# Dense stages: the weight split placed behind a step's transpositions, and the second pair scaled in two steps

## Chip, cores and metric

The kernel runs on one core of one Trainium2 chip. The metric is the device time of one execution in microseconds (us); the time before is the median of three runs. One further execution was recorded by the hardware profiler; all durations below come from it. Five engines work side by side, each through its own list of instructions in order: TensorE (PE: matrix products and transpositions, results in PSUM), VectorE (DVE), ScalarE (ACT), GpSimd (POOL) and SyncE (SP, which issues most transfers). They wait for one another by semaphores.

## The reference

An encoder of two layers over 1024 tokens of width 1024, in fp32: layer 0 mixes tokens by a 2-D neighbourhood attention, layer 1 by a grouped-query attention. The change lies where the output projection of a mixer ends and the gate product begins:

```python
        x = x + y
        g = jax.nn.sigmoid(rms_norm(x, ple_norm_g[i]) @ ple_w_gate[i])
        x = x + g * (p[i] @ ple_w_proj[i])
    return rms_norm(x, final_norm_g)
```

`rms_norm(x, g)` is x times the reciprocal root of the mean of its squares, times a gain. y is the mixer's output; its last step is the output projection, `(o * jax.nn.silu(gate)) @ w_out`.

## The kernel before

**Numbers in two parts.** Every matrix product is made of three: each operand is split into a high part (a rounded copy, made on ACT) and a low part (operand less high part, made on DVE), and `split3` (its matmuls stand at L352) adds high x high, high x low and low x high. HTh and HTl are the two parts of the transposed activations, tile t of 128 tokens in eight chunks of 128 columns; wh and wl are those of one unit of weights (128 x 1024), whose raw form lies in a staging tile (wstage, two of them).

**The dense stage** (`dense_phase`, once behind each mixer, so twice in the program) does the output product, the residual, a norm, and the gate product. The output product is a Strassen form of seven products instead of eight (`strassen_out`). Its last part is a loop of eight steps, numbered n = 0 to 7 here, which `dense_phase` drives at L1831. In a step PE does one block of twelve 128x512 matmuls; then DVE adds the block's PSUM tile to half of a tile X of the residual (`fold`, L1691), ACT squares that half and sums it (`square`, L1777), and these follow in the order written:

- `WQ.pump()`: DVE makes the low part wl of the weight unit begun one pump earlier (`settle`, L246), SP issues the load of a further unit, and ACT makes the high part wh of the next unit (L241). Here the units are the four of the gate product's first half.
- `norms[n]`: pieces of the norm. `prep` (L1807, n = 1), `powers` (L1787 and a power on POOL, n = 2, 4, 7), `roots` (L385 to L387, n = 3, 5, 8), `scale_pair` (L1802, n = 3, 5, 9, 11), which writes the normed tiles xn of two token tiles m and 4 + m. Pair 0 (tiles 0 and 4) is scaled in step 3 as four pieces of 512 columns, pair 1 (tiles 1 and 5) in step 5 as two whole tiles of 1024.
- `pend_ht(True)`: up to two entries of a list are taken. Each one (`to_ht`, L530) is four PE transpositions of 128 columns from xn into one of four PSUM tiles t (L534), a copy to HTh on ACT (L535) and the subtraction into HTl on DVE (L536). An entry is due three steps behind its scaling for the first half of the columns, four for the second. So PE has a group of eight transpositions, four of each tile of a pair, behind the blocks of steps 5 and 6 (pair 0), 7 and 8 (pair 1), then 11 and on.

Steps from n = 8 on belong to the gate product (L1930 and on); blocks 8 and 9 use weight units 0 and 1 with the first halves of token tiles 0 and 4, blocks 10 and 11 units 2 and 3 with their second halves. That loop is not touched.

**What sets the order.** The program is scheduled by hand: each engine gets its instructions in the order in which the Python code issues them, and takes them strictly in that order.

Of the kernel before, what the change touches and what calls it, by code (L numbers as in the profile page):

```python
# [16 lines left out]
ALU = mybir.AluOpType  # L17
# [148 lines left out]
def trunk(ctx, tc, x, wts, rpb, gains, hgains, mask, sides, rope, gain0, out):  # L166
    nc = tc.nc
    sync, act, dve, pool, pe = nc.sync, nc.scalar, nc.vector, nc.gpsimd, nc.tensor
# [125 lines left out]
    WQ = Weights()  # L294
# [213 lines left out]
    def load_gain(pl, i, bufs):  # L508
        gt = pl.tile([128, D], F32, name="gain", bufs=bufs)
        sync.dma_start(gt, bcast(gains, i * D, D))  # L510
        return gt
# [18 lines left out]
    def to_ht(pt, t, xn, cs=(0, 1)):  # L530
        for c in cs:
            ps = pt.tile([128, 4, 128], F32, name="t")
            for k in range(4):
                pe.transpose(ps[:, k], xn[:, (4 * c + k) * 128:(4 * c + k + 1) * 128], ident)  # L534
            act.activation(HTh[:, t, 4 * c:4 * c + 4], ps, AF.Copy)  # L535
            dve.tensor_tensor(HTl[:, t, 4 * c:4 * c + 4], ps, HTh[:, t, 4 * c:4 * c + 4], ALU.subtract)  # L536
# [1205 lines left out]
    def dense_phase(l):  # L1742
        with ExitStack() as es:
# [4 lines left out]
            X = [one.tile([128, D], F32, name=f"X{t}") for t in range(NT)]  # L1748
# [10 lines left out]
            def xalloc():  # L1759
                return sb.tile([128, D], F32, name="xn", bufs=4)  # L1760

            def salloc():
                return stg.tile([128, D], F32, name="wstage")

            def pend_ht(pairs=False):
                clock[0] += 1
                for _ in range(2 if pairs else 1):
                    if pend and pend[0][0] <= clock[0]:
                        to_ht(ps_t, *pend.pop(0)[1:])
# [4 lines left out]
            def square(t, c):  # L1774
                i = 2 * (t % 4) + t // 4
                cs = slice(512 * c, 512 * c + 512)
                act.activation(junk[:, cs], X[t][:, cs], AF.Square, accum_out=sa[:, c, i:i + 1])  # L1777

            rn = {}
# [11 lines left out]
            def roots(m, k):  # L1791
                r = sb.tile([128, 4], F32, name="rn", bufs=4)[:, :2 * k]
                root_step(r, *half_roots.pop(m))
                for i in range(k):
                    rn[m + i] = r[:, 2 * i:2 * i + 2]

            def scale_pair(m, age=3):
                xs = [(t, xalloc()) for t in (m, 4 + m)]
                n = 512 if m == 0 else 1024
                for c in range(0, 1024, n):  # L1800
                    for i, (t, xn) in enumerate(xs):
                        dve.scalar_tensor_tensor(xn[:, c:c + n], X[t][:, c:c + n], rn[m][:, i:i + 1], g1[:, c:c + n],  # L1802
                                                 op0=ALU.mult, op1=ALU.mult)
                pend.extend([(clock[0] + age + c, t, xn, (c,)) for c in range(2) for t, xn in xs])

            def prep():
# [3 lines left out]
                1: [prep],  # L1810
                2: [lambda: powers(0, 1)],
                3: [lambda: roots(0, 1), lambda: scale_pair(0)],
                4: [lambda: powers(1, 1)],
                5: [lambda: roots(1, 1), lambda: scale_pair(1)],
                7: [lambda: powers(2, 2)],
                8: [lambda: roots(2, 2)],
                9: [lambda: scale_pair(2)],
                11: [lambda: scale_pair(3)],
            }
# [11 lines left out]
            for n, (step, m) in enumerate(strassen_out(l, X, ps_d, ps_t, early)):  # L1831
                if n == 0:
                    sb = es.enter_context(tc.tile_pool(name="dsb", bufs=2))
                    wp4 = es.enter_context(tc.tile_pool(name=f"wp4{l}", bufs=2))
                    WQ.alloc[4] = lambda: [wp4.tile([128, 1024], F32R, name=f"w{c}4") for c in "hl"]
                    WQ.cap[4] = 2
                    g1 = load_gain(sb, 2 * l + 1, 2)
                    g2 = load_gain(sb, 2 * l + 2, 2)
                    WQ.age, WQ.lag, age, lag = 1, 0, WQ.age, WQ.lag
                square(m + 4 if step == 5 else m, 1)  # L1840
                WQ.pump()
                for f in norms.get(n, ()):
                    f()
                pend_ht(True)
            WQ.age, WQ.lag = 2, 2

            for kind in ("ple",):
# [3 lines left out]
                for hf in range(2):  # L1851
# [77 lines left out]
                    for t, i in order:  # L1929
# [31 lines left out]
                        xn = salloc() if l == 0 and t >= 6 else xalloc()  # L1961
# [40 lines left out]
    ropeD = dram.tile([2, NT, 128, 2, 64], F32, name="ropeD")  # L2002
    mixer_a()
    pend = dense_phase(0)
    mixer_b(pend)
    dense_phase(1)


# [16 lines left out]
```

## Time and profile before

| | us |
|---|---|
| Median of 3 runs (lowest to highest) | 1480.99 (1480.89 to 1481.51) |
| The profiled execution's time | 1481.56 |
| Its span, first to last instruction | 1479.8 |
| ACT busy in the span | 914.3 (62%) |
| POOL busy in the span | 430.7 (29%) |

The first dense stage's eight steps lie at about 571 to 594 us of the span, the second's at about 1360 to 1383. In a row of the timeline the first number is the start in us from the span's start, the second how long the row lasts; then engine, line, operation, tile written <- tiles read, shape, and how many instructions the row holds; in brackets is the idle time ahead of it on its engine, and who ended it. A PE instruction's recorded time runs into the next one's, so PE's pace is read from start to start.

### The profile page before, as it was taken

The numbers are of one execution on the slowest core, as the hardware profiler recorded it, in microseconds if no ns is written. First come the engines' busy times: TensorE is split into PE (matmuls) and PEld (weight loads), VectorE is DVE, ScalarE is ACT, GpSimd is POOL, SyncE is SP. The second block draws the span as 40 slices with busy tenths as digits, with TensorE's granted clock in tenths as the row PEclk, the third lists the DMA queues.
The fourth block names the chain that finished last, engine by engine and source line by source line (L and its number), as shares of the span: only waits on it lengthen the run. The fifth ranks groups of instructions, "written<-read, shape, count | busy, mean of one in ns | idle before, by whom it ended". The sixth has DMA issues, their size and how long they took to land.

```text
span 1479.8 us, 23443 instructions
## 1 busy us (share of the span) xinstructions
PE 1467.4 (99%) x8305; PEld 1272.1 (86%) x8305; DVE 1071.4 (72%) x1943; ACT 914.3 (62%) x1836; POOL 430.7 (29%) x623
## 2 busy tenths in 40 slices
PE   9999999999999999999999999999999999999997
PEld 7888888988988887888888888999999988888886
DVE  5468776487487598656767787877878787789845
ACT  5477776477477635443456777777767777744522
POOL 3245764275244200020154342424141400000010
PEclk9999999999999999999999999999999999999999
DMA  7324564373122863262120111101101122763223
GB/s 248 116 89 160 108 161 139 72 167 98 36 90 86 327 256 100 86 197 102 61 86 12 40 51 46 42 17 55 46 28 60 42 65 65 256 242 108 78 93 129
DMA packets 91605, 157.62 MB, mean 107 GB/s; under 512 B 18272, under 2 KB 54368, under 8 KB 90976
## 3 DMA queue, kind: packets, MB, share of 16 engines
q1 hardware_dynamic: 87776, 144.71, 29.2%
q0 software_dynamic: 2560, 8.39, 3.7%
q10 hardware_dynamic: 1152, 3.02, 0.7%
q8 instruction: 66, 1.08, 0.3%
q14 instruction: 51, 0.42, 0.1%
HBM read 125.56 MB, written 50.83 MB: 119 GB/s over the span
## 4 chain that ended last, share of the span: by engine, by line
PE 58%; DVE 2%; ACT 1%; issue 0%; POOL 0%; ACTq 0%; POOLq 0%; DVEq 0%
PE d L352 29%; PE s L352 11%; PE o L352 9%; PE t L1446 7%; PE t L534 1%; PE t L352 1%; PE t L1398 0%; DVE xn L1802 0%; DVE X L1691 0%; DVE wl L1589 0%; DVE PTl L1449 0%; DVE mn L1428 0%; DVE HTl L1637 0%; ACT junk L1777 0%; DVE X L1644 0%
## 5 line engine op out<-in xcount | busy, mean ns | idle before, releaser
L352 PE MATMUL d<-wh,HTh 128*128 128x512 f32 (+1 forms) x800 | 285.5, 358 | 0.3 <-ACT G L688 0.2
L352 PE MATMUL d<-wh,HTl 128*128 128x512 f32 (+1 forms) x800 | 282.7, 355 | 0.2 <-DVE HTl L536 0.2
L352 PE MATMUL d<-wl,HTh 128*128 128x512 f32 (+1 forms) x800 | 281.6, 354 | 0.2 <-DVE stat L942 0.2
L1449 DVE TENSOR_TENSOR PTl<-t,PTh 128x512 fp32r<-128x512 f32 x256 | 164.6, 685 | 105.1 <-ACT PTh L1448 104.5
L352 PE MATMUL d<-HTh,wh 128*128 128x512 f32 x480 | 193.8, 404 | 0.0
L352 PE MATMUL d<-HTh,wl 128*128 128x512 f32 x480 | 188.7, 393 | 0.0
L352 PE MATMUL d<-HTl,wh 128*128 128x512 f32 x480 | 188.1, 392 | 0.0
L352 PEld LDWEIGHTS d<-wh,HTh 128*128 128x128 f32 x800 | 150.5, 189 | 22.7 <-ACT G L688 0.5
L352 PEld LDWEIGHTS d<-wh,HTl 128*128 128x128 f32 x800 | 150.8, 189 | 22.3 <-DVE HTl L536 0.5
L352 PEld LDWEIGHTS d<-wl,HTh 128*128 128x128 f32 x800 | 150.8, 189 | 22.3 <-POOL wl L261 0.5
L1434 ACT ACTIVATE P<-s,mn 128x1024 f32<-128x1024 f32 x128 | 143.0, 1117 | 37.8 <-DVE mn L1428 36.7
L1448 ACT ACTIVATE PTh<-t 128x512 fp32r<-128x512 f32 x256 | 138.6, 594 | 43.4 <-PE t L1446 42.1
L1428 DVE TENSOR_REDUCE mn<-s 128x1 f32<-128x1024 f32 x128 | 154.8, 1209 | 5.7 <-PE s L352 5.3
L886 POOL TENSOR_TENSOR PTh<-PTh,SIDE 128x256 fp32r<-128x256 f32 x96 | 80.8, 842 | 201.9 <-ACT PTh L881 201.9
L352 PE MATMUL s<-KA,QS 128*128 128x512 f32 (+2 forms) x384 | 134.8, 405 | 0.0
L1446 PE MATMUL t<-ident,P 128*128 128x128 f32 x1024 | 133.3, 273 | 0.4 <-DVE PTl L1449 0.4
L1446 PEld LDWEIGHTS t<-ident,P 128*128 128x128 f32 x1024 | 116.7, 141 | 9.6 <-DVE PTl L1449 2.1
L352 PE MATMUL s<-KB,QS 128*128 128x512 f32 (+2 forms) x384 | 121.4, 370 | 0.0
L352 PE MATMUL o<-PTl,V 128*128 128x256 f32 (+2 forms) x672 | 119.9, 290 | 0.0
L352 PE MATMUL o<-PTh,V 128*128 128x256 f32 (+2 forms) x672 | 118.1, 287 | 0.7 <-DVE Y L557 0.3
L246 DVE TENSOR_TENSOR wl<-wstage,wh 128x1024 fp32r<-128x1024 f32 x75 | 92.4, 1235 | 27.4 <-ACT wh L241 27.2
L352 PEld LDWEIGHTS d<-HTh,wl 128*128 128x128 f32 x480 | 90.1, 188 | 20.3
(296 smaller groups left out, 2911.4 us busy)
## 6 DMA issues: line engine op xcount, KB each, us to landing
wstage<-in_wts SPq DMA_DIRECT2D x87, 512.0 KB
pp<-ppD SPq DMA_DIRECT2D x32, 256.0 KB
X<-in_x SPq DMA_DIRECT2D x15, 512.0 KB
rb<-rD SPq DMA_DIRECT2D x58, 128.0 KB
tD0t<-in_wts SPq DMA_DIRECT2D x16, 256.0 KB
tD1t<-in_wts SPq DMA_DIRECT2D x16, 256.0 KB
ppD<-th SPq DMA_DIRECT2D x16, 256.0 KB
xD<-X SPq DMA_DIRECT2D x8, 512.0 KB
```

Source lines behind the costliest of these rows:

```text
L246: eng.tensor_tensor(lo[:, c:c + n], s[:, c:c + n], hi[:, c:c + n], ALU.subtract)
L352: pe.matmul(ps, a, b, start=first, stop=last, skip_group_check=True)
L534: pe.transpose(ps[:, k], xn[:, (4 * c + k) * 128:(4 * c + k + 1) * 128], ident)
L886: pool.tensor_tensor(pt[:, 3 * j - 1:3 * j + 4:4], pt[:, f1:f1 + 1].to_broadcast([128, 2, 128]), SIDE[:, :2], ALU.mult)
L1428: dve.tensor_reduce(mn, ps, axis=AX.X, op=ALU.min)
L1434: act.activation(p, ps, AF.Exp, bias=mn, scale=-1.0, accum_out=RS[h, hf][:, t:t + 1])
L1446: pe.transpose(ps[:, i], p[:, k * 128:(k + 1) * 128], ident)
L1448: act.activation(PTh[:, ks, c], ps, AF.Copy)
L1449: dve.tensor_tensor(PTl[:, ks, c], ps, PTh[:, ks, c], ALU.subtract)
```

## The change

In each of the eight steps the pump comes last, behind the step's norm pieces and its transpositions. And of pair 1 only tile 1 is scaled in step 5; the scaling of tile 5 is put off to step 6, behind that step's transpositions and ahead of its pump. No instruction is added or taken away, and the entries for the transpositions keep their steps.

```diff
--- before.py
+++ after.py
@@ -1794,13 +1794,22 @@
                 for i in range(k):
                     rn[m + i] = r[:, 2 * i:2 * i + 2]
 
+            rest = []
+
             def scale_pair(m, age=3):
                 xs = [(t, xalloc()) for t in (m, 4 + m)]
                 n = 512 if m == 0 else 1024
+
+                def scaled(i, c):
+                    t, xn = xs[i]
+                    dve.scalar_tensor_tensor(xn[:, c:c + n], X[t][:, c:c + n], rn[m][:, i:i + 1], g1[:, c:c + n],
+                                             op0=ALU.mult, op1=ALU.mult)
                 for c in range(0, 1024, n):
-                    for i, (t, xn) in enumerate(xs):
-                        dve.scalar_tensor_tensor(xn[:, c:c + n], X[t][:, c:c + n], rn[m][:, i:i + 1], g1[:, c:c + n],
-                                                 op0=ALU.mult, op1=ALU.mult)
+                    for i in range(2):
+                        if m == 1 and i == 1:
+                            rest.append(lambda: scaled(1, 0))
+                        else:
+                            scaled(i, c)
                 pend.extend([(clock[0] + age + c, t, xn, (c,)) for c in range(2) for t, xn in xs])
 
             def prep():
@@ -1838,10 +1847,14 @@
                     g2 = load_gain(sb, 2 * l + 2, 2)
                     WQ.age, WQ.lag, age, lag = 1, 0, WQ.age, WQ.lag
                 square(m + 4 if step == 5 else m, 1)
-                WQ.pump()
+                more = rest[:]
+                del rest[:]
                 for f in norms.get(n, ()):
                     f()
                 pend_ht(True)
+                for f in more:
+                    f()
+                WQ.pump()
             WQ.age, WQ.lag = 2, 2
 
             for kind in ("ple",):
```

PE's list and SP's list hold the same instructions in the same order as before, and so does POOL's. The order changes on DVE and ACT alone, in the same way in both dense stages; shown is the first (X_5832 to X_5839 are the residual's tiles 0 to 7; the numbers on wh and wl are those of tile allocations, rising in the order of the weight units).

On DVE in steps 1 to 3 (the rows of L1691 are the folds of steps 2 and 3):

```order
+L1816 TENSOR_SCALAR sa<-sa 128x8
 L246 TENSOR_TENSOR wl_6307<-wstage,wh_6306 128x1024
-L1807 TENSOR_SCALAR sa<-sa 128x8
 L1691 TENSOR_TENSOR X_5832<-d,X_5832 128x512
-L246 TENSOR_TENSOR wl_6328<-wstage,wh_6327 128x1024
 L1787 SCALAR_TENSOR_TENSOR sa<-sa 128x2
+L246 TENSOR_TENSOR wl_6329<-wstage,wh_6328 128x1024
 L1691 TENSOR_TENSOR X_5838<-d,X_5838 128x512
```

`prep` moved ahead of the first unit's wl, and the sum of `powers` in step 2 ahead of the second unit's wl, which now stands right ahead of the fold of step 3.

On DVE from the roots of step 5 to the fold of step 7 (the first two rows are `roots` of step 5, L1691 with X_5834 is the fold of step 6; the pairs of L536 are the HTl of steps 5 and 6):

```order
 L386 SCALAR_TENSOR_TENSOR wkn<-wkn,sa 128x2
 L387 SCALAR_TENSOR_TENSOR rn<-wkn 128x2
-L1802 SCALAR_TENSOR_TENSOR xn<-X_5833,rn,gain 128x1024
-L1802 SCALAR_TENSOR_TENSOR xn<-X_5837,rn,gain 128x1024
+L1805 SCALAR_TENSOR_TENSOR xn<-X_5833,rn,gain 128x1024
 L536 TENSOR_TENSOR HTl<-t,HTh 128x512 x2
 L1691 TENSOR_TENSOR X_5834<-d,X_5834 128x512
-L246 TENSOR_TENSOR wl_6409<-wstage,wh_6408 128x1024
 L536 TENSOR_TENSOR HTl<-t,HTh 128x512 x2
+L1805 SCALAR_TENSOR_TENSOR xn<-X_5837,rn,gain 128x1024
+L246 TENSOR_TENSOR wl_6430<-wstage,wh_6429 128x1024
 L1691 TENSOR_TENSOR X_5835<-d,X_5835 128x512
```

The scaling of tile 5 (X_5837) moved from behind that of tile 1 to behind four HTl and a fold; the third unit's wl moved behind it.

On ACT from the square of step 5 to that of step 7 (the rows of L1777):

```order
 L1777 ACTIVATE junk,sa<-X_5839 128x512
-L241 ACTIVATE wh_6408<-wstage 128x1024
-L535 ACTIVATE HTh<-t 128x512 x2
+L535 ACTIVATE HTh<-t 128x512 x2
+L241 ACTIVATE wh_6429<-wstage 128x1024
 L1777 ACTIVATE junk,sa<-X_5834 128x512
-L241 ACTIVATE wh_6448<-wstage 128x1024
-L535 ACTIVATE HTh<-t 128x512 x2
+L535 ACTIVATE HTh<-t 128x512 x2
+L241 ACTIVATE wh_6462<-wstage 128x1024
 L1777 ACTIVATE junk,sa<-X_5835 128x512
```

In steps 5 and 6 the high part of a weight unit, wh, moved from ahead of the two HTh copies to behind them.

## The prediction

> **What bounds the kernel now.** First the page's span and its busy line, then the list of who waited for whom, cut to PE and to the first dense stage's steps.
>
> ```profile
> span 1479.8 us, 23443 instructions
> PE 1467.4 (99%) x8305; PEld 1272.1 (86%) x8305; DVE 1071.4 (72%) x1943; ACT 914.3 (62%) x1836; POOL 430.7 (29%) x623
> PE t L534 <- DVE HTl L536: 0.6, 2, 0.4
> ```
>
> PE is busy 99% of the span, so any time that PE stands still in the change's stages is added to the end, and any wait taken away comes off it. The third row is all that the trace names as PE waiting in the first stage: 0.6 us, for HTl to free a PSUM tile. In the second stage the same list is empty. So there is little to win; the question is what PE waits for afterwards. The chain of waits shows how that 0.6 us arises in the first stage:
>
> ```profile
> 592.16 0.95 ACT wh L241
> 593.11 0.49 ACT HTh L535
> 593.60 0.02 issue
> 593.62 0.70 DVE HTl L536
> 594.33 0.04 issue
> 594.37 1.25 PE t L534 x8
> ```
>
> The split of a weight unit (wh) stands on ACT ahead of the HTh copy, DVE's HTl follows, and PE's group of step 8 waits for the PSUM tile. From the end of a DVE instruction (594.32) to PE it takes 0.05 us. PE's timeline, first stage, then second:
>
> ```profile
> 590.20 1.25 PE L534 MATMUL t<-ident,xn 128*128 128x128 f32 x8 [0.36 <-DVE HTl L536]
> 591.21 0.48 PE L352 MATMUL d<-wh,HTh 128*128 128x512 f32 x1
> 595.38 0.47 PE L352 MATMUL d<-wh,HTh 128*128 128x512 f32 x1
> ...
> 1378.80 1.04 PE L534 MATMUL t<-ident,xn 128*128 128x128 f32 x8
> 1379.59 0.48 PE L352 MATMUL d<-wh,HTh 128*128 128x512 f32 x1
> 1383.24 0.48 PE L352 MATMUL d<-wh,HTh 128*128 128x512 f32 x1
> ```
>
> In the second stage the group of step 7 takes 0.79 us (1378.80 to 1379.59), and block 8 with its group 3.65 (1379.59 to 1383.24): this is the pace without waits. In the first stage the same two take 1.01 and 4.17, and 0.36 is lost ahead of them. So the first stage loses 0.36 + 0.22 + 0.52 = 1.1 us here, the second nothing.
>
> **The change part by part.** Nothing is added or removed; everything is a matter of when DVE and ACT reach an instruction. DVE's timeline in the second stage, and ACT's:
>
> ```profile
> 1364.51 1.23 DVE L246 TENSOR_TENSOR wl<-wstage,wh 128x1024 fp32r<-128x1024 f32 x1 [2.27 <-ACT wh L241]
> 1366.33 1.22 DVE L246 TENSOR_TENSOR wl<-wstage,wh 128x1024 fp32r<-128x1024 f32 x1
> 1367.46 0.15 DVE L1787 SCALAR_TENSOR_TENSOR sa<-sa 128x2 f32<-128x2 f32 x1
> 1368.48 0.16 DVE L385 TENSOR_TENSOR wkn<-wkn 128x2 f32<-128x2 f32 x1 [0.26 <-POOL wkn L376]
> 1369.07 2.74 DVE L1802 SCALAR_TENSOR_TENSOR xn<-X,rn,gain 128x512 f32<-128x512 f32 x4
> 1371.72 0.69 DVE L1691 TENSOR_TENSOR X<-d,X 128x512 f32<-128x512 f32 x1
> 1373.26 0.16 DVE L1787 SCALAR_TENSOR_TENSOR sa<-sa 128x2 f32<-128x2 f32 x1 [0.85 <-ACT junk L1777]
> 1373.33 0.69 DVE L1691 TENSOR_TENSOR X<-d,X 128x512 f32<-128x512 f32 x1
> 1374.82 2.48 DVE L1802 SCALAR_TENSOR_TENSOR xn<-X,rn,gain 128x1024 f32<-128x1024 f32 x2
> 1377.21 1.28 DVE L536 TENSOR_TENSOR HTl<-t,HTh 128x512 fp32r<-128x512 f32 x2
> 1378.41 0.68 DVE L1691 TENSOR_TENSOR X<-d,X 128x512 f32<-128x512 f32 x1
> 1379.01 1.22 DVE L246 TENSOR_TENSOR wl<-wstage,wh 128x1024 fp32r<-128x1024 f32 x1
> 1381.38 1.29 DVE L536 TENSOR_TENSOR HTl<-t,HTh 128x512 fp32r<-128x512 f32 x2 [1.15 <-ACT HTh L535]
> ```
>
> ```profile
> 1372.50 0.63 ACT L1777 ACTIVATE junk<-X 128x512 bf16<-128x512 f32 x1 [3.47 <-DVE X L1691]
> 1379.19 0.63 ACT L1777 ACTIVATE junk<-X 128x512 bf16<-128x512 f32 x1 [2.43 <-DVE X L1691]
> 1379.82 1.05 ACT L241 ACTIVATE wh<-wstage 128x1024 fp32r<-128x1024 f32 x1
> 1380.77 1.06 ACT L535 ACTIVATE HTh<-t 128x512 fp32r<-128x512 f32 x2
> ```
>
> The spacings, start to start: wl to the next DVE instruction 1.13 (1366.33 to 1367.46); fold to ACT's square 0.78 (1371.72 to 1372.50); square to `powers` 0.76 (1372.50 to 1373.26); `powers` to the next 0.07; fold to the next 0.60 (1378.41 to 1379.01); `roots` to scaling 0.59 (1368.48 to 1369.07); two whole scalings 2.39 (1374.82 to 1377.21), so one 1.20, and it ends 1.28 after its start; two HTl 1.20 (1377.21 to 1378.41); square to the next on ACT 0.63 (1379.19 to 1379.82); HTh to HTl 0.61 (1380.77 to 1381.38).
>
> *Part 1, the pump behind the norm pieces (steps 1 to 3).* It looks free and is not. Before, DVE made the second unit's wl while ACT squared; now `powers` stands ahead of it, so DVE waits for ACT first and makes wl afterwards. First wl 1364.51; fold of step 2 at 1365.64; square 1366.42; `powers` 1367.18; second wl 1367.25; fold of step 3 at 1368.38; `roots` 1368.98 (POOL's power, at most 1.02 behind `powers`, is there by 1368.20); scaling of pair 0 at 1369.57 instead of 1369.07. So the norm runs 0.50 us later, not earlier. In the second stage PE is past caring: its group of step 5 starts well behind the scaling. If POOL's power should be slower beside a running wl, it has 0.78 us in hand.
>
> *Part 2, tile 5 put off.* From pair 0's scaling to tile 1's the list is unchanged, 5.75 us (1369.07 to 1374.82): tile 1 is scaled at 1375.32. Then HTl of step 5 at 1376.52 (its HTh is early: fold 1373.83, square 1374.61, HTh 1375.24, and HTl could run at 1375.85), fold of step 6 at 1377.72. Here DVE sends ACT to work and needs it back: square 1378.50, HTh of step 6 at 1379.13, HTl 1379.74 and one more, **scaling of tile 5 at 1380.94**, ended 1382.22. Before, it had ended at 1377.30 (1374.82 and 2.48). PE takes tile 5's transpositions in the group of step 7, as before: the group starts at 1378.80, its first four (tile 1) are through at 1379.20, and the second four wait until 1382.27. **The wait is 3.1 us.** Behind it in PE's list stand block 8 and everything after; PE reaches block 8 at 1382.7 instead of 1379.59.
>
> In the first stage DVE begins this list at
>
> ```profile
> 576.65 1.23 DVE L246 TENSOR_TENSOR wl<-wstage,wh 128x1024 fp32r<-128x1024 f32 x1 [2.27 <-ACT wh L241]
> ```
>
> that is 787.86 us ahead of the second stage's 1364.51. The same steps end tile 5's scaling at 594.36; PE goes on at 594.41, the last four transpositions take 0.40, block 8 and its group 3.65: block 9 starts at 598.5 instead of 595.38, **3.1 us later**. PE itself stands still for some 3.8 us there: the group starts at about 590.2 as before, its first four are through at 590.6, and the next comes at 594.41. The 1.1 us lost before lie inside, so they are not lost again.
>
> *Part 3, wh behind HTh on ACT.* This does what the chain above suggests: HTh comes 0.95 us sooner after its square, and PSUM tiles come free sooner (HTl of step 6 at 1379.74 instead of 1381.38). It takes away the first stage's 1.1 us, which is already counted, since the 3.1 compares block 9 with block 9. What is late next is the weights: units 2 and 3 are read by block 10. The third wl follows tile 5 at 1382.14, then the fold of step 7 (1383.27), square (1384.05), `powers` (1384.81), HTl (1385.3 and 1385.9), last wl 1386.5 to 1387.7. Block 10 starts at about 1389.1 now that PE waits: 1.4 us in hand, so I cost it at nothing. Without that cover it is up to the same 1.4 us again. SP's loads keep their order; the buffer for the fourth unit comes free 0.9 us later (wl at 1367.25 instead of 1366.33), its wh runs at 1380, over ten us later.
>
> Sum of the waits: 3.1 + 3.1 = **6.2 us**.
>
> *Part 4, PE's clock in a wait.* No wait of this length lies inside the trace before, so its price is bounded. The end of the run shows PE after its last matmul, and the stretches of the span show the granted clock (the column ahead of the last two):
>
> ```profile
> 1.35 1.97 PE L968 MATMUL gain<-ident 128*128 128x128 f32 x8 [1.35 <-POOL ident masks.py:199]
> 7.15 0.66 PE L534 MATMUL t<-ident,X 128*128 128x128 f32 x4 [0.17 <-DVE X L960]
> 1471.97 0.28 PE L352 MATMUL d<-wh,HTl 128*128 128x256 f32 x1
> 1472.00:1474.00 2.00, 0.24 (x3) 0.05 (x1) 1.39 (x5) 1.90 (x5) 0.00 (x0) 1.00 0.57 231
> 1474.20:1474.40 0.20, 0.00 (x0) 0.00 (x0) 0.05 (x1) 0.12 (x1) 0.00 (x0) 0.50 0.03 0
> ```
>
> The last matmul ends at 1472.25, and from 1474.2 the clock is half: **two us of standing still were enough** once. And it does not come back at once: at the start eight transpositions took 1.97 us, against 1.04 at 1378.80, and the pace was full only by 7.15, 5.8 us after the first one. So after a wait of 3 us or more the work may run at half pace for between 0 and 5.8 us, which loses 0 to 2.9 us in a stage. I take the middle, 1.45 a stage, **2.9 in all**: the end of the run is the nearest row and speaks for a loss, and how long it lasts is open. Below nothing it cannot be.
>
> [...]
>
> Together 6.2 + 2.9 = 9.1 us. Against the profiled execution's own 1481.56 that is 1490.7; that execution lies 0.57 above the median of the three runs, and on the median it is 1480.99 + 9.1 = **1490.1 us**.
>
> **The rivals.**
> 1. *The clock stays up.* The waits come as computed, PE resumes at full pace: 1480.99 + 6.2 = 1487.2. For it: the waits are only 3.1 and 3.8 us. Against: the clock at the end of the run.
> 2. *Tile 5 in time, so not slower.* PE waits for nothing, and the first stage's 1.1 us go: 1480.99 - 1.1 = 1479.9, which is within 0.2% (3.0 us, about what a measurement here can tell from no change). It decides at 1379.20: tile 5's scaling would have to end by then instead of 1382.22, 3.0 us sooner. For it: HTh of step 6 could follow PE's group of step 6 closely, as PSUM is ready early. Against: the list above is bound to DVE and ACT handing X and its square to each other, not to PE, and DVE has only 1.4 us of waiting in it behind tile 1.
> 3. *Only one stage waits,* or each half as long, because a handover is quicker where the list has changed: 1480.99 + 3.1 = 1484.1. For it speaks only that my spacings come from other neighbours.
>
> **How the numbers follow.** Waits in both stages and the clock falling in at least one: 0.60, 1490.1. Rival 1: 0.25, 1487.2. Rival 2: 0.08. Rival 3: 0.07, where also more than the forecast may be hidden. The range goes from 1485.5 (rival 1 with waits a quarter shorter) to 1493.0 (6.2 and twice 2.9 are 1493.1) and leaves out rivals 2 and 3. Faster by over 0.2% would need 3 us won where PE waits 1.1: 0.02. Within 0.2%: 0.08. Slower: 0.90.
>
> **What would show it.** In the profile after: PE waiting in the middle of the group of step 7, for xn from the scaling, 3 us in the second stage and nearly 4 in the first; pair 0's scaling 5.06 us behind the first wl's start instead of 4.56, HTl of step 6 right behind an HTh that follows its square by 0.63; the granted clock at 0.5 for some us from block 8 on; no wait at block 10. It is wrong if the scaling of tile 5 starts before 1378 (shifted by what the first stage lost), or if PE waits at another place.

## The result, and the profile after

| | before | changed |
|---|---|---|
| Median, us (lowest to highest) | 1481.25 (1480.89 to 1481.60), 4 runs | 1491.27 (1488.83 to 1491.98), 4 runs |
| Ratio, with its 95% interval | | 1.0065 (1.0053 to 1.0076) |
| Profiled execution, us | 1481.56 | 1491.98 |
| Its span, us | 1479.8 | 1490.2 |

The changed kernel is 10.0 us slower. From the page of the changed kernel its span, and from the list of who waited for whom the first row for PE (us in total, times, longest):

```profile
span 1490.2 us, 23441 instructions
...
PE t L534 <- DVE xn L1805: 6.9, 2, 3.8
```

Two waits, one in each dense stage, in PE's transpositions (L534) for a scaled tile xn (L1805 is the scaling's line now). Such a row was not there before. PE's timeline shows where they lie, first stage, then second:

```profile
589.76 0.60 PE L534 MATMUL t<-ident,xn 128*128 128x128 f32 x4
594.19 1.09 PE L534 MATMUL t<-ident,xn 128*128 128x128 f32 x4 [3.83 <-DVE xn L1805]
594.93 0.78 PE L352 MATMUL d<-wh,HTh 128*128 128x512 f32 x1
...
600.91 0.48 PE L352 MATMUL d<-wh,HTh 128*128 128x512 f32 x1
...
1384.34 0.60 PE L534 MATMUL t<-ident,xn 128*128 128x128 f32 x4
1387.99 0.64 PE L534 MATMUL t<-ident,xn 128*128 128x128 f32 x4 [3.06 <-DVE xn L1805]
1388.38 0.69 PE L352 MATMUL d<-wh,HTh 128*128 128x512 f32 x1
...
1393.60 0.48 PE L352 MATMUL d<-wh,HTh 128*128 128x512 f32 x1
```

The group of step 7 is torn in two: four transpositions of tile 1, a wait, four of tile 5. The last row of each part is the start of block 9. Why tile 5 comes late is read from DVE's timeline in the second stage, and ACT's beside it:

```profile
1370.05 1.23 DVE L246 TENSOR_TENSOR wl<-wstage,wh 128x1024 fp32r<-128x1024 f32 x1 [1.39 <-ACT wh L241]
1375.20 2.74 DVE L1805 SCALAR_TENSOR_TENSOR xn<-X,rn,gain 128x512 f32<-128x512 f32 x4
1380.95 1.28 DVE L1805 SCALAR_TENSOR_TENSOR xn<-X,rn,gain 128x1024 f32<-128x1024 f32 x1
1382.15 1.28 DVE L536 TENSOR_TENSOR HTl<-t,HTh 128x512 fp32r<-128x512 f32 x2
1383.35 0.68 DVE L1691 TENSOR_TENSOR X<-d,X 128x512 f32<-128x512 f32 x1
1385.37 1.29 DVE L536 TENSOR_TENSOR HTl<-t,HTh 128x512 fp32r<-128x512 f32 x2 [1.33 <-ACT HTh L535]
1386.57 1.27 DVE L1805 SCALAR_TENSOR_TENSOR xn<-X,rn,gain 128x1024 f32<-128x1024 f32 x1
```

```profile
1384.12 0.63 ACT L1777 ACTIVATE junk<-X 128x512 bf16<-128x512 f32 x1 [1.24 <-DVE X L1691]
1384.75 1.07 ACT L535 ACTIVATE HTh<-t 128x512 fp32r<-128x512 f32 x2
```

The fold of step 6 (1383.35) releases ACT's square, HTh follows it at once, DVE stands idle for 1.33 us until HTh is there, does HTl, and only then scales tile 5. Its start is 16.52 us behind the first wl (1370.05 to 1386.57).

The waits name 6.9 of some 10.4 us. The rest is pace. The stretches of the span, with the granted clock in the column ahead of the last two:

```profile
590.00:593.10 3.10, 0.36 (x4) 0.12 (x2) 1.77 (x4) 2.64 (x5) 0.00 (x0) 1.00 0.00 0
593.20:599.90 6.70, 5.71 (x16) 4.67 (x17) 5.46 (x10) 1.69 (x4) 1.01 (x1) 0.50 0.00 0
600.00:605.00 5.00, 5.00 (x27) 4.22 (x26) 3.62 (x5) 1.09 (x2) 0.00 (x0) 1.00 0.00 0
...
1388.50:1391.80 3.30, 3.30 (x10) 2.58 (x9) 2.13 (x5) 1.69 (x4) 1.01 (x1) 0.50 0.02 5
1392.00:1396.00 4.00, 4.00 (x24) 3.35 (x23) 3.65 (x8) 1.08 (x2) 0.00 (x0) 1.00 0.00 0
```

In both stages the granted clock is 0.50 from about the end of the wait: some 6.8 us in the first stage, of which 5.8 hold work, and 3.4 in the second. So the 10.4 us split like this, block 9 against block 9 (in the profile before at 595.38 and 1383.24). First stage: PE goes on at 594.19; at full pace 0.40 for the four transpositions and 3.65 for block 8 and its group would bring block 9 at 598.24, 2.86 late; it comes at 600.91, so 2.67 more is the clock. Second stage, with 5.53 carried over: 1387.99 and the same 4.05 make 1392.04 against 1388.77, 3.27 for the wait; block 9 comes at 1393.60, 1.56 for the clock. Waits 6.13, clock 4.23, together 10.36; the spans differ by 10.4.

### The profile page after: what moved, and what is told of

Read it like the earlier page. It is cut to its first block, busy times and chain, and to the rows that moved or that the text cites. A ratio compares the mean times of both kernels' runs of the same rounds, so it can differ in the third digit from the quotient of the medians.

```text
span 1490.2 us, 23441 instructions
## 1 busy us (share of the span) xinstructions
PE 1471.0 (99%) x8305; PEld 1275.4 (86%) x8305; DVE 1071.0 (72%) x1943; ACT 914.2 (61%) x1836; POOL 430.8 (29%) x623
## 4 chain that ended last, share of the span: by engine, by line
PE 57%; DVE 4%; ACT 1%; issue 0%; POOL 0%; ACTq 0%; DVEq 0%
PE d L352 28%; PE s L352 11%; PE o L352 9%; PE t L1446 7%; PE t L534 1%; PE t L352 1%; DVE xn L1805 1%; DVE X L1691 1%; PE t L1398 0%; ACT junk L1777 0%; DVE HTl L536 0%; DVE X L1644 0%; DVE wl L246 0%; DVE wl L1589 0%; DVE HTl L1637 0%
```

## Experiments

Theory A is this account. Rival P says that moving the pump costs, rival B that the time behind the wait has nothing to do with the clock. All times are medians in us; the time of the kernel before was 1481.17 in the first four experiments, 1481.25 in the next four, 1481.14 in the last.

**e0_change: the changed kernel again.**

> The changed kernel again, for the spread of its executions. Theory A (two waits of PE for tile 5's scaling, 3.1 and 2.9 us, and then half the clock for a stretch whose length differs from one execution to the next): between 1487.2 (the waits alone, 1481.25 + 6.0) and about 1493, median near 1491, and the spread over 2 us against 0.7 before; shorter executions have the higher mean clock. Theory B (no clock in it, work behind the wait is slow for another reason): the spread is as narrow as before, 0.7 us.

Measured: 1491.12 (1490.84 to 1491.94, 5 runs), ratio 1.0069 (1.0056 to 1.0082). The spread here is 1.1 us, not over 2; only with the four runs of above, one of which took 1488.83, it is 3.2, against 0.8 for the kernel before. So the scatter speaks for A, but weakly. The mean granted clock of these nine runs speaks for it more clearly, since it falls as the time rises: 0.998 in the run of 1488.83, 0.997 in the four from 1490.73 to 1491.12, 0.996 in the four from 1491.65 on. In this execution's first stage the half clock lasts half as long as in the profile above (over 3.2 us, against 6.8), although the wait has the same 3.8 us:

```profile
594.90:598.10 3.20, 3.20 (x10) 2.59 (x9) 2.03 (x5) 1.69 (x4) 0.82 (x1) 0.50 0.00 0
598.30:600.00 1.70, 1.70 (x12) 1.44 (x11) 1.67 (x4) 0.02 (x1) 0.00 (x0) 1.00 0.00 0
```

**e1_pump_last: the pump's move alone.** Against the kernel before:

```diff
                 square(m + 4 if step == 5 else m, 1)
-                WQ.pump()
                 for f in norms.get(n, ()):
                     f()
                 pend_ht(True)
+                WQ.pump()
```

> Only the pump goes to the step's end; both tiles of the second pair are scaled in step 5 as before. Theory A: tile 5 is ready in time, no wait for its scaling, so about the time before, 1481.25, at most 1 us to either side (the norm runs 0.5 us later, the HTh copies 0.95 us sooner). Rival P (moving the pump is what costs, since the weights' low parts and the norm come later): most of the 10 us, over 1486.

Measured: 1482.00 (1481.64 to 1482.31, 11 runs), ratio 1.0005 (0.9997 to 1.0014). Rival P falls: the pump's move accounts for 0.8 us of the 10 at the medians, and the interval still holds 1. A part of it is lost where the prediction had reckoned with a cover of 1.4 us that only a wait of PE gives. The list of waits, for PE's weight loads in the second stage, has the one row

```profile
PEld d L352 <- DVE wl L246: 0.5, 1, 0.5
```

Block 10 stands ready before the last wl is made; the first stage has the same wait of 0.5 us. Where PE waits 3 us for tile 5, this is hidden.

**e2_put_off: tile 5's scaling put off alone.** Against the changed kernel:

```diff
                 more = rest[:]
                 del rest[:]
+                WQ.pump()
                 for f in norms.get(n, ()):
                     f()
                 pend_ht(True)
                 for f in more:
                     f()
-                WQ.pump()
```

> Only tile 5's scaling is put off to step 6; the pump stays ahead of the norm pieces. Theory A: the waits are there in full and some 0.7 us longer in each stage, since wl and wh now stand ahead of the HTl for which the scaling queues: 3.8 and 3.6 us, so 1488.7 with the full clock and about 1492 to 1493 with the clock lost as in the changed kernel. Rival P: near 1481.25.

Measured: 1492.77 (1492.60 to 1493.74, 5 runs), ratio 1.0081 (1.0067 to 1.0095). This part alone brings the whole loss, and more. PE's timeline, the second halves of the torn groups:

```profile
594.77 1.09 PE L534 MATMUL t<-ident,xn 128*128 128x128 f32 x4 [5.06 <-DVE xn L1805]
...
1388.96 1.09 PE L534 MATMUL t<-ident,xn 128*128 128x128 f32 x4 [3.70 <-DVE xn L1805]
```

The second stage waits 3.70, expected 3.8. The first waits 5.06, expected 3.6: there PE comes to the group sooner, because pair 0's scaling does not run 0.5 us later as it does with the pump behind, and the expectation had counted block 9's delay there, not the standing still.

**e3_fill13: work of no use in the place of the wait.** Against the changed kernel:

```diff
-    def to_ht(pt, t, xn, cs=(0, 1)):
+    def to_ht(pt, t, xn, cs=(0, 1), fill=0):
         for c in cs:
             ps = pt.tile([128, 4, 128], F32, name="t")
+            for _ in range(fill):
+                mm(ps, HTh[:, 7, 0, :], HTh[:, 7, 0:4, :], True, True)
...
-                        to_ht(ps_t, *pend.pop(0)[1:])
+                        e = pend.pop(0)[1:]
+                        to_ht(ps_t, *e, fill=13 if clock[0] == 8 and e[0] == 5 else 0)
```

> The changed kernel with thirteen 128x512 matmuls of no use ahead of tile 5's transpositions in step 7, into the PSUM tile that these then overwrite: 13 x 0.227 = 2.95 us of work in the place of the wait. Theory A: the waits are filled, the clock stays full behind them, block 8 takes 2.85 us, and the time is the waits alone, 1481.25 + 6 to 7 = 1487 to 1488, spread under 1 us: faster with more work. Theory B: the time stays at 1491, block 8 stays slow.

Measured: 1487.86 (1487.59 to 1488.18, 5 runs), ratio 1.0046 (1.0033 to 1.0058). With 26 matmuls more the kernel is 3.3 us faster than the changed one (1491.12), and its spread is 0.6 us. PE's timeline in the first stage, and the stretch around it:

```profile
590.62 3.24 PE L352 MATMUL t<-HTh 128*128 128x512 f32 x13
594.61 0.66 PE L536 MATMUL t<-ident,xn 128*128 128x128 f32 x4 [0.76 <-DVE xn L1808]
595.03 0.48 PE L352 MATMUL d<-wh,HTh 128*128 128x512 f32 x1
```

```profile
590.00:600.00 10.00, 9.24 (x49) 7.46 (x48) 7.49 (x12) 5.43 (x11) 1.01 (x1) 1.00 0.00 0
```

The granted clock is 1.00 all through, and the last four transpositions take 0.42 (594.61 to 595.03), where they took 0.74 in the changed kernel (594.19 to 594.93). Rival B falls. The waits cost 6.7 us (1487.86 less 1481.17), the clock 3.3 us in the median.

**e6_fill6: half as much of it.** As e3, with six matmuls instead of thirteen.

> The changed kernel with six useless matmuls in the wait instead of thirteen (1.36 us), so that PE stands still for about 1.7 us in the second stage and 2.4 in the first. It asks from what length of wait the clock is lost. If some two us in one stretch of the throttle are enough (as at the end of the run before): the first stage loses the clock in some executions, 1487.2 to 1490. If a longer standstill is needed: 1487.2 in all, spread under 1 us.

Measured: 1488.93 (1487.29 to 1489.52, 5 runs), ratio 1.0049 (1.0036 to 1.0062). Two runs lie at 1487.3 and 1487.5, three between 1488.9 and 1489.5. In the profiled one, from PE's timeline and by stretches:

```profile
593.98 1.12 PE L536 MATMUL t<-ident,xn 128*128 128x128 f32 x4 [2.36 <-DVE xn L1808]
...
1386.54 0.66 PE L536 MATMUL t<-ident,xn 128*128 128x128 f32 x4 [1.58 <-DVE xn L1808]
```

```profile
594.00:597.30 3.30, 3.30 (x10) 2.82 (x11) 2.13 (x4) 1.55 (x4) 0.48 (x1) 0.50 0.00 0
597.40:600.00 2.60, 2.60 (x17) 2.23 (x16) 2.41 (x6) 0.61 (x3) 0.43 (x1) 1.00 0.00 0
1383.00:1390.00 7.00, 5.42 (x29) 4.27 (x28) 4.82 (x7) 4.09 (x9) 0.62 (x1) 1.00 0.00 0
```

In this execution the clock was lost behind the wait of 2.36 us and kept behind that of 1.58. The two shorter runs point to a clock kept in both stages: their mean granted clock is 0.999, that of the three longer ones 0.998 and 0.997, and 3.41 us at half would take an estimated 0.0011 off the mean (half of 3.41 in 1487). Their times fit that too (the waits alone make 1487.9 in e3).

**e5_ahead: tile 5 put off, but ahead of step 6's transpositions.** Against the changed kernel:

```diff
-                pend_ht(True)
                 for f in more:
                     f()
+                pend_ht(True)
                 WQ.pump()
```

> The changed kernel, with tile 5's scaling ahead of step 6's transpositions instead of behind them, so that it no longer queues behind ACT's square and HTh copy. Theory A: its scaling starts some 2.6 us sooner; PE's waits shrink to about 0.4 us in the second stage and 1.2 in the first, too short for the clock: 1481.25 + 0.5 + 0.5 = 1482.2, between 1481 and 1483. Rival (splitting the pair over two steps costs as such): no less than 1487.

Measured: 1482.36 (1482.11 to 1482.98, 11 runs), ratio 1.0008 (0.9999 to 1.0017), expected 1482.2. PE's waits for the scaling, first stage and second:

```profile
PE t L534 <- DVE xn L1805: 1.2, 1, 1.2
...
PE t L534 <- DVE xn L1805: 0.4, 1, 0.4
```

Both are as expected, 1.2 and 0.4 us, and block 8 runs at full pace behind them (2.83 and 2.84 us; the mean granted clock of this execution is 0.999). It is the queue behind HTl that costs, not that the pair is scaled in two steps.

**e4_due_later and e7_before_due_later: the second pair's transpositions one step later.** In the changed kernel and in the kernel before:

```diff
-                5: [lambda: roots(1, 1), lambda: scale_pair(1)],
+                5: [lambda: roots(1, 1), lambda: scale_pair(1, 4)],
```

> The changed kernel, with the transpositions of the second pair due one step later (steps 8 and 9). Theory A: PE has a block of 2.8 us more ahead of them, so the 3 us wait is all but gone and the clock stays: the first stage's 1.1 us of before goes too, 1480.2, between 1479.9 and 1481.2. Rival P (the pump's move costs by itself): above 1486.

> The kernel before, with only the transpositions of the second pair due one step later. Theory A: the first stage's waits at the groups of steps 7 and 8 go (1.1 us in the profile of before): 1480.2. If the pump's move is worth something by itself, e4 is below this one; if it costs its 0.5 us of later norm on PE, e4 is above; I expect the two within 0.5 us.

Measured: e4 1483.05 (1482.87 to 1483.57, 11 runs), ratio 1.0013 (1.0004 to 1.0021); e7 1480.90 (1480.55 to 1481.23, 11 runs), ratio 0.9998 (0.9989 to 1.0006). A block in the wait's place takes 8 of the 10 us away, as A has it, but e4's figure was missed by 2.9 us, and the two are not within 0.5; e7 itself was expected at 1480.2. A block is 2.8 us, the first stage's wait 3.8, so 1.1 is left in e4:

```profile
PE t L534 <- DVE xn L1805: 1.1, 1, 1.1
...
PE t L534 <- DVE xn L1805: 0.3, 1, 0.3
```

And the wait moves on to the group of step 13 in the first stage, for HTl that is queued behind the fourth pair's scaling. In e4 it shows only among PE's weight loads (0.7 us in two waits); in e7 this is PE's only named wait in the stage:

```profile
PE t L534 <- DVE HTl L536: 0.4, 1, 0.4
```

**e8_both_later: the fourth pair a step later as well.** As e7, with `scale_pair(3, 4)` too.

> The kernel before with the transpositions of the second and of the fourth pair due one step later. With the second pair alone later, the profile shows a new wait of 0.4 us at the group of step 13 (HTl queued on DVE behind the fourth pair's scaling; the block and the group take 0.7 us more than without waits). Theory A: a block more in between takes it away as well, 0.7 us off 1480.9: about 1480.2 to 1480.5. If the wait only moves on again: 1480.9.

Measured: 1480.26 (1479.82 to 1480.87, 11 runs), ratio 0.9993 (0.9984 to 1.0002). The profile names no wait of PE in either stage any more. All eleven runs are at or below the fastest of the fifteen of the kernel before (1480.87), and the medians differ by 0.9 us; the interval still holds 1, so it is a gain of under 0.2% at best, and not a proven one.

## Why the prediction was right, point by point

- **The late scaling (part 2).** Predicted to start 16.43 us behind the first wl, measured 16.52; the waits 3.1 and 3.8 us, measured 3.06 and 3.83. The steps in between came as the spacings had it: DVE needs ACT's square and HTh back before it may scale. e2 and e5 show that this place in DVE's list is the cause.
- **The norm's delay (part 1).** Pair 0's scaling 5.06 us behind the first wl instead of 4.56; measured 5.15 (1370.05 to 1375.20). Nothing is won by it anywhere. The prediction speaks only of the second stage here. In the first, PE's group of step 5 follows the start of this scaling by 0.85 us in both kernels, and in the changed one PE stands still for 0.47 us ahead of it; the wait for tile 5 hides that, in e1 nothing does.
- **wh behind HTh, and the cover of the weights (part 3).** HTh did follow its square by 0.63 (1384.12 to 1384.75). The cover was the weak point, as said there: in e1, without the wait, block 10 waits for wl. One reading in this part was too good: in e1 the first stage's 1.1 us go only in part. The 0.36 us ahead of the group of step 7 stays, and block 9 comes 0.40 us sooner than before (594.98 against 595.38). The sum does not rest on it, as it compares block 9 with block 9.
- **Sum of the waits.** 6.2 predicted; 6.13 by the two profiles, 6.7 by e3 (with 0.76 of a wait still in its first stage).
- **The clock (part 4).** Both stages lost it, behind waits of 3.83 and 3.06 us; in e6 it fell behind one of 2.36 too. 2.9 us was taken, from a range of 0 to 5.8: the profiled execution shows 2.67 and 1.56, the medians of e0 and e3 differ by 3.3. The size was the middle of a wide range, which no row of the profile before narrowed; that it came so near is luck, and it was a little low. That the clock would fall at all was argued from a row, and that held. Rival 1, the clock staying up, was 1487.2: e3 came near it by work (1487.86), and so did one run of the changed kernel with 1488.83, whose mean granted clock was 0.998, against 0.996 in the profiled one with its 10.24 us at half in the two stages.
- **Rivals 2 and 3** did not come about. Rival 2 needed tile 5 some 3 us sooner; e5, which moves it ahead of one HTh handover, wins 2.6 of that (a wait of 0.43 in place of 3.06 in the second stage) and comes out within 1.1 us of the kernel before.

## What to carry to other kernels

Before an instruction is moved behind another one on a busy engine, follow what that other one waits for: here a scaling of 1.2 us was put behind two HTl that need an answer from a second engine, and its reader found it 3 us late. On a kernel whose PE is busy 99% of the time, a new wait of PE can cost its length and then some: here the granted clock was 0.50 behind waits of 2.36, 3.06 and 3.83 us, which by the profile of the changed kernel added 1.56 us to the second of them and 2.67 to the third, and the times scattered. A slack in the schedule that comes from a wait elsewhere is gone when that wait is mended.

## What was not expected of the hardware

- In the traces of the kernel before and of the changed one the granted clock changes, from the first entry of its record on, only at whole multiples of 3.413 us. In the kernel before it is full for 1467.73 us (430 of them), then half; in the changed one full for 587.09 (172), half for 6.83 (2), full for 788.48 (231), half for 3.413 (1), full for 95.57 (28), then half. The rows below are stretches of this length, by PE's busy time (the first number behind the length): three of e6, the last one with matmuls of the kernel before, two of e7 at the end of its matmuls and the clock behind them, then the same of the changed kernel.

```profile
590.52:593.93 3.41, 1.10 (x5) 0.56 (x3) 2.49 (x4) 2.32 (x5) 0.00 (x0) 1.00 0.00 0
1382.41:1385.82 3.41, 2.55 (x14) 1.78 (x12) 2.08 (x4) 2.64 (x5) 0.00 (x0) 1.00 0.00 0
1385.82:1389.23 3.41, 2.69 (x14) 2.31 (x15) 2.56 (x4) 0.92 (x3) 0.00 (x0) 1.00 0.00 0
1470.78:1474.19 3.41, 1.47 (x13) 1.27 (x12) 2.73 (x10) 2.99 (x6) 0.00 (x0) 1.00 0.39 156
1470.43:1473.84 3.41, 1.47 (x13) 1.27 (x12) 2.72 (x10) 2.99 (x6) 0.00 (x0) 1.00 0.39 156
1473.84:1477.25 3.41, 0.00 (x0) 0.00 (x0) 1.34 (x5) 0.92 (x2) 0.00 (x0) 1.00 0.24 88
1477.30:1478.30 1.00, 0.00 (x0) 0.00 (x0) 0.00 (x0) 0.00 (x0) 0.00 (x0) 0.50 0.57 209
1480.63:1484.04 3.41, 2.00 (x18) 1.80 (x16) 2.62 (x10) 2.48 (x5) 0.16 (x1) 1.00 0.23 94
1484.05:1487.46 3.41, 0.00 (x0) 0.00 (x0) 1.85 (x7) 1.43 (x4) 0.00 (x0) 1.00 0.22 87
1487.50:1489.00 1.50, 0.00 (x0) 0.00 (x0) 0.00 (x0) 0.00 (x0) 0.00 (x0) 0.50 0.74 277
```

The clock fell at the end of the first, the fourth and the sixth row, where PE stood still for 2.31, 1.94 and 3.41 us. It stayed full behind the second, third and fifth: 0.86, 0.72 and, in e7, 1.94 again. e6's wait of 1.58 us lies in two of the rows. In the changed kernel's rows it stayed full behind 1.41 us and fell behind 3.41, and in its two dense stages it fell behind stretches with 2.80 and 2.93 us of standing still. Every other such stretch at full clock in the traces of these two kernels, from the first entry on, has less than 0.6 us of it, and none of them lost the clock. The length of the standing still alone did not decide: counted from the end of the last matmul, the clock fell after 1.94 us in the kernel before (1472.25 to 1474.19) and after 4.83 in the changed one (1482.63 to 1487.46). No run tested by itself what does.

- In the changed kernel the half clock lasted 6.83 us in the first stage, where PE stood still for the first 1.02 us of it (half from 593.17, PE on at 594.19), and 3.41 us in the second, where PE was at work all through. The longer one cost 2.67 us, the shorter 1.56.
- Useless matmuls made a kernel faster: 26 of them took 3.3 us off (e3, 1487.86 against 1491.12).
